# Second sums ahead of the seventh weight step, placed queries rounded behind the eighth

## The chip, the cores and the metric

The kernel runs on one core of one Trainium2 chip. The metric is the device time of one execution in microseconds (us). Its engines are TensorE (PE; PEld is its weight load), VectorE (DVE), ScalarE (ACT), GpSimd (POOL) and SyncE (SP); the last two are used here almost only to issue transfers.

## The reference, cut to what matters

A trunk of four layers works on x of 256 positions by 2048 features, in float32. Each layer has one mixer of the kinds 0, 1, 2, 0. Kinds 1 and 2 are the "grouped" layers that the change concerns: 32 query heads share 4 key and value heads of width 64; kind 1 attends to 64 selected keys per query, kind 2 to a window of 128.

```python
h = _rmsnorm(x, norm_in[i])
self_out, mq, gate = mixer(h @ w_in)                  # 2048 wide, 1024, 3072
mem_out = _memory_attention(mq, mem_n @ w_mem_kv[i])  # 4 heads of 256
y = concat([self_out, mem_out]) * silu(gate)          # 3072 wide
x = x + y @ w_out[i]
```

## The kernel before

**Products in two halves.** Each float32 operand is split into a rounded high part and the rest. For a weight tile `wr` ScalarE writes `wh` (L58) and VectorE writes `wl` (L71), in `split_in_order`; TensorE then makes three products, x high by `wh`, x high by `wl`, x low by `wh` (L241 to L243 in `rows_by`). A "weight step" is 1024 columns of weights on 128 partitions (two contraction tiles of 512 columns): one transfer of 512 KB on SP's queue, one `wh`, one `wl` and 12 matmuls of 512 columns. A product over 2048 features takes eight steps, called s = 0, 2, 4, ..., 14 in the code; so s = 12 is the seventh and s = 14 the eighth. There are five buffers for `wr` and three each for `wh` and `wl`.

**The order of a grouped layer.** Parts are worked in the order 4, 0, 1, 2, 3, 5; parts 4 and 5 are the memory heads, parts 0 to 3 the four groups g of eight query heads. For a group: the queries (`rows_by` "q", eight steps), the gate (`gate_by_rows`, `rows_by` "gr", eight steps), then the output product of the part before (`w_out`, "wo", four chunks of two steps). The sums of values of a part are made while the part after it has its queries and its gate computed, in four pieces called `steps`: `parts(0)`, first sums, `parts(1)`, second sums. `parts` rounds the turned softmax weights (tiles `pL` and `vz`, with high part `pH`). The sums of one half are 12 matmuls into tile `o` (`mo` for the memory heads); `paired` (or `gated`) multiplies them by the gate on VectorE (`yt`) and splits the product on ScalarE and VectorE (`y`).

**Queries are placed through DRAM.** The query accumulators go through `qz`, `qT`, a transfer `placed<-qT` and eight transfers `qR<-placed`, all issued by POOL, four for each half z. `parts_q(z)` then rounds the placed half `qR` to `qS` (ScalarE, then VectorE on 64 partitions). Scores (`sp`, three matmuls of 256 columns for a head, six for a pair of heads) read `qS`; softmax, its transposes and POOL's transfers `turn<-T`, `pL<-turn`, `vz<-turn` follow.

**What sets the order.** The program is traced in Python order; a planner then orders the instructions of each engine by its own simulated times, and each engine runs its list strictly in that order. `tc.keep_in_program_order` keeps the planner from moving an instruction, and `tc.issue_after(ins)` puts an instruction behind `ins` on the same engine. `split_in_order` uses the list `behind`: the next `wh` and `wl` are issued after whatever stands in it. `hooks` of `rows_by` maps a step to functions that are traced behind that step's matmuls.

Before the change, the gate of a group had these hooks (L965, L966), and `parts_q` put both halves into `behind`:

```python
hooks = {2: [lambda: behind.extend(ahead)], 10: steps[2:3], 12: steps[3:] + [lambda: parts_q(0), pairs[0]],
         14: [lambda: parts_q(1)] + pairs[1:]}
```

So second sums and the rounding of the first placed half were traced behind step 12, and the `wh` of step 14 was issued behind the latter. Where the second sums' matmuls fell among those of the weight steps was left to the planner.

Of the kernel before, what the change touches and what calls it, by code (L numbers as in the profile page):

```python
# [15 lines left out]
P = 128  # L16
S = 256
# [15 lines left out]
def kernel(ctx: ExitStack, tc: tile.TileContext, a: dict, out: bass.AP,  # L33
                             kinds=(0, 1, 2, 0)):
    nc = tc.nc
# [28 lines left out]
    behind = []  # L64
# [156 lines left out]
    def accumulators(name):  # L221
        return ps.tile([P, 2, 512], F32, name=f"acc_{name}", tag="acc", bufs=2)

    def rows_by(xt, kts, w, k0, cols, name, hooks={}, opening=False):

        acc = accumulators(name)
        n = cols[1] if len(cols) == 2 else cols[1] * cols[4]
        step = 4 if n <= 256 else ST
        for s in range(0, kts, step):
            wr, n = stage(w, k0 + s, step, cols)  # L230
            if opening:
                for f in hooks[s]:
                    f()
            wh, wl = parts_of(wr, step * n, n if opening and s < 8 else None)
            for k in range(step):
                q = xt[(s + k) // 4]
                at = slice(k * n, (k + 1) * n)
                for t in range(2):
                    xh, xl = (q[:, v, (s + k) % 4, t * P:(t + 1) * P] for v in range(2))
                    first, last = s + k == 0, s + k == kts - 1  # L240
                    nc.tensor.matmul(acc[:, t, :n], xh, wh[:, at], start=first, stop=False)  # L241
                    nc.tensor.matmul(acc[:, t, :n], xh, wl[:, at], start=False, stop=False)  # L242
                    nc.tensor.matmul(acc[:, t, :n], xl, wh[:, at], start=False, stop=last)  # L243
            for f in () if opening else hooks.get(s, ()):
                f()
        return acc
# [213 lines left out]
            copy_act(dst(i0, i1), f32(tp)[:, :(i1 - i0) * P].rearrange("p (j c) -> p j c", c=P))  # L460


    def gate(nm, w, c0, hooks={}):
        gT = None
        for h in range(2):
            z = total(columns_by(nm.at, 16, w, 0, (c0 + h * S, S), "g", {} if h else hooks))
            if gT is None:
                gT = act.tile([P, 4, S], F32, name="gT", tag="gT", bufs=1)
            nc.vector.tensor_mul(z, z, nm.half[:, None, :].to_broadcast([P, 2, S]))
            th = gT[:, 2 * h:2 * h + 2, :]  # L470
            nc.scalar.activation(th, z, AF.Tanh)
            nc.vector.scalar_tensor_tensor(th, th, 1.0, z, op0=OP.add, op1=OP.mult)
        return gT


    def gate_by_rows(nm, w, c0, hooks={}):
        acc = rows_by(nm.at, 16, w, 0, (c0, 512), "gr", hooks)
        gT = act.tile([P, 8, 4, 32], F32, name="gTr", tag="gT", bufs=1)
        d = dr.tile([2, P, 512], F32, name="turned", tag="turned", bufs=4)
        for t in range(2):  # L480
# [127 lines left out]
    def memory_project(nm, i, w, mq0, g0, part, steps, deferred):  # L608
# [7 lines left out]
        for h in range(2):  # L616
# [12 lines left out]
            head_parts(q, acc)  # L629
            qT.append(q)  # L630
        return (nm, kT, v, qT), lambda: gate(
            nm, w, g0 + 2048 + part * 512, {8: steps[2:3], 12: steps[3:]} if deferred else {})

    def memory_attend(nm, kT, v, qT):
        ws = []
# [25 lines left out]
        def sums(h, y, gT, p_s):  # L661
            pH, pL = p_s
            o = misc("mo")
            for j in range(2):
                c = (2 * h + j) * P
                seq = [(v[z][:, t, c:c + P], p_[:, t * S:(t + 1) * S])
                       for t in range(2) for z, p_ in ((0, pH), (0, pL), (1, pH))]
                for n_, (l, r_) in enumerate(seq):
                    nc.tensor.matmul(o[:, j * S:(j + 1) * S], l, r_, start=n_ == 0, stop=n_ == 5)
            gated(y, o, gT, 2 * h)  # L670
        return Sums([ws[:1], ws[1:]], lambda h, y, gT, p_s: sums(h, y, gT, p_s[0]))


# [158 lines left out]
    class Grouped:  # L832
# [108 lines left out]
        def project(self, g, steps):  # L941
# [14 lines left out]
            def parts_q(z):  # L956
                r4 = raw[z][:].rearrange("p (t m b) -> p m t b", m=4, b=32)
                one = tc.keep_in_program_order(copy_act(quads(q[z]), r4))
                two = nc.vector.tensor_sub(quads(q[z])[64:], r4[64:], quads(f32(q[z]))[64:])
                behind.extend((one.ins, two.ins))  # L960
            if g == 0:
                self.load_biases(0, 0)
                self.load_biases(0, 1)
            pairs, sums = self.attend(g, q)
            hooks = {2: [lambda: behind.extend(ahead)], 10: steps[2:3], 12: steps[3:] + [lambda: parts_q(0), pairs[0]],  # L965
                     14: [lambda: parts_q(1)] + pairs[1:]}  # L966
            if g < 3:
                for s_, half in ((4, 0), (14, 1)):
                    hooks.setdefault(s_, []).append(lambda half=half: self.load_biases(g + 1, half))
            return sums, gate_by_rows(nm, self.w, self.g0 + g * 512, hooks)  # L970

        def load_biases(self, g, half):
            bm = act.tile([P, 4, S], F32, name="bm", tag="aux", bufs=AUX)
# [9 lines left out]
        def attend(self, g, q):  # L983
# [28 lines left out]
            def sums(z, y, gT, p_s):  # L1012
                o = misc("o")
                for u in range(2):
                    pp = p_s[u]
                    v0 = g * P + (64 if u == 0 else 0)
                    for t in range(2):
                        for n_, (x_, p_) in enumerate(((0, 0), (0, 1), (1, 0))):
                            nc.tensor.matmul(o[:, t * S:], self.vz[x_][:, t, v0:v0 + P],
                                             pp[p_][:, 512 * t:512 + 256 * t],  # L1020
                                             start=u == t == n_ == 0, stop=u == t == 1 and n_ == 2)
                paired(y, o, gT, 2 * z)
            order = (0, 2, 1, 3, 4, 6, 5, 7)

            def pair(m):
# [197 lines left out]
```

## Time and profile before

| | |
|---|---|
| median of 3 runs | 2578.14 us (2577.4 to 2580.79) |
| the profiled execution | 2578.37 us, of which the span from first to last instruction is 2576.6 us |
| TensorE busy | 2531.9 us, 98% of the span |
| mean granted TensorE clock | 0.992 |
| VectorE, ScalarE, POOL busy | 71%, 55%, 16% |
| HBM traffic | 236 GB/s over the span |

Busy shares are means over stages with different limits. In the rows below a time is us from the span's start, the second number of a timeline row is its length in us, and square brackets hold the idle time of the engine ahead of the row and what ended it. A clock of 1.00 is 2.4 GHz, the lower level is 1.2 GHz, and a value between says that a stretch holds both.

### The profile page before, as it was taken

Reading aid. Unit: us, or ns where it says so; the run is one execution under the profiler, and the core shown is the slowest. Engines: PE = TensorE matmul, PEld = TensorE weight load, DVE = VectorE, ACT = ScalarE, POOL = GpSimd, SP = SyncE. Lnnn points to the kernel's source line nnn. Section 1 sums busy time; section 2 is a strip of 40 time slices with the busy share of each in tenths; the row PEclk is TensorE's granted clock in tenths of the full one; section 3 lists DMA queues with packets and bytes.
Section 4 is the critical chain, followed back from the end, with each engine's and each line's share of the span. In section 5 each row is a group of like instructions: output and inputs, shape, how many; then the busy total and the mean of one; then the engine's idle time right before and its main releaser. Section 6 shows DMA issues by size and latency. Waiting matters only on the chain.

```text
span 2576.6 us, 38117 instructions
## 1 busy us (share of the span) xinstructions
PE 2531.9 (98%) x13336; PEld 2176.3 (84%) x13336; DVE 1823.0 (71%) x3074; ACT 1418.0 (55%) x2236; POOL 402.5 (16%) x649
## 2 busy tenths in 40 slices
PE   8999999999999999999999999999999999999998
PEld 7888888888888889877787888777788888888887
DVE  6565656677676685877787775877787667777767
ACT  6454546555455454556566554665565555455554
POOL 1000000111111100112332101222230011111110
PEclk9999999999999999999999999999999999999999
DMA  9889888877887757678888677788894887888874
GB/s 311 275 276 310 279 283 242 211 208 206 222 224 229 217 175 210 204 217 246 265 270 231 203 240 213 244 244 236 255 255 149 243 210 207 210 220 219 249 214 151
DMA packets 462399, 597.26 MB, mean 232 GB/s; under 512 B 78768, under 2 KB 306752, under 8 KB 461056
## 3 DMA queue, kind: packets, MB, share of 16 engines
q1 hardware_dynamic: 419856, 464.46, 60.3%
q0 software_dynamic: 41344, 129.47, 17.9%
q8 instruction: 105, 1.72, 0.3%
q10 hardware_dynamic: 1008, 0.91, 0.1%
q14 instruction: 86, 0.70, 0.1%
HBM read 536.30 MB, written 71.01 MB: 236 GB/s over the span
## 4 chain that ended last, share of the span: by engine, by line
PE 93%; DMA 4%; issue 1%; DVE 1%; POOL 1%; ACT 1%; ACTq 0%; SPq 0%; DVEq 0%; POOLq 0%
PE acc_wo L242 7%; PE acc_wo L243 7%; PE acc_wo L241 7%; PE acc_mq L265 5%; PE acc_mk L265 5%; PE acc_g L265 5%; PE acc_gr L242 4%; PE acc_gr L241 4%; PE acc_gr L243 4%; PE acc_cq L265 3%; PE acc_qn L265 3%; PE acc_mv L241 2%; PE acc_mq L267 2%; PE acc_g L267 2%; PE acc_mv L242 2%; PE acc_mk L267 2%
## 5 line engine op out<-in xcount | busy, mean ns | idle before, releaser
L71 DVE TENSOR_TENSOR wl<-wr,wh 128x1024 fp32r<-128x1024 f32 (+2 forms) x860 | 1028.2, 1197 | 539.5 <-ACT wh L58 530.1
L58 ACT ACTIVATE wh<-wr 128x1024 fp32r<-128x1024 f32 (+2 forms) x860 | 891.2, 1038 | 837.8 <-PE acc_wo L243 167.8
L241 PE MATMUL acc_wo<-wh,y 128*128 128x512 f32 x752 | 293.5, 390 | 0.0
L242 PE MATMUL acc_wo<-wl,y 128*128 128x512 f32 x752 | 293.5, 390 | 0.0
L243 PE MATMUL acc_wo<-wh,y 128*128 128x512 f32 x752 | 293.4, 390 | 0.0
L241 PE MATMUL acc_gr<-wh,xT 128*128 128x512 f32 x512 | 206.6, 403 | 26.7 <-ACT wh L58 26.7
L242 PE MATMUL acc_gr<-wl,xT 128*128 128x512 f32 x512 | 205.3, 401 | 1.3 <-DVE wl L71 1.3
L243 PE MATMUL acc_gr<-wh,xT 128*128 128x512 f32 x512 | 205.1, 401 | 0.0
L241 PEld LDWEIGHTS acc_wo<-wh,y 128*128 128x128 f32 x752 | 141.3, 188 | 29.0
L242 PEld LDWEIGHTS acc_wo<-wl,y 128*128 128x128 f32 x752 | 141.3, 188 | 28.2
L243 PEld LDWEIGHTS acc_wo<-wh,y 128*128 128x128 f32 x752 | 141.2, 188 | 27.8
L265 PE MATMUL acc_mq<-xT,wh 128*128 128x512 f32 x512 | 162.0, 396 | 0.0
L265 PE MATMUL acc_g<-xT,wh 128*128 128x512 f32 x512 | 161.4, 395 | 0.0
L265 PE MATMUL acc_mk<-mT,wh 128*128 128x512 f32 x512 | 160.8, 395 | 0.0
L544 POOL DMA_DIRECT2D pL<-turn x192 | 120.7, 635 | 201.9 <-DMA turn<-T 95.8
L241 PEld LDWEIGHTS acc_gr<-wh,xT 128*128 128x128 f32 x512 | 99.8, 195 | 48.5 <-ACT wh L58 28.3
L1127 DVE TENSOR_TENSOR x<-x,acc_wo 128x1024 f32<-128x1024 f32 x92 | 111.7, 1214 | 17.5 <-PE acc_wo L243 17.5
L539 POOL DMA_DIRECT2D turn<-T x56 | 42.7, 763 | 502.5 <-DVE T L533 468.9
L265 PE MATMUL acc_qn<-cT,wh 128*128 128x512 f32 x384 | 120.6, 395 | 0.0
L265 PE MATMUL acc_cq<-xT,wh 128*128 128x512 f32 x384 | 120.6, 395 | 0.0
L242 PEld LDWEIGHTS acc_gr<-wl,xT 128*128 128x128 f32 x512 | 100.0, 195 | 22.3 <-DVE wl L71 2.3
L243 PEld LDWEIGHTS acc_gr<-wh,xT 128*128 128x128 f32 x512 | 99.2, 194 | 20.3
(331 smaller groups left out, 5327.1 us busy)
## 6 DMA issues: line engine op xcount, KB each, us to landing
wr<-in_w_out_dram SPq DMA_DIRECT2D x192, 512.0 KB, 4.6
wr<-in_w_in_a_dram SPq DMA_DIRECT2D x176, 512.0 KB, 4.5
wr<-in_w_mem_kv_dram SPq DMA_DIRECT2D x128, 512.0 KB, 5.6
wr<-in_w_in_b_dram SPq DMA_DIRECT2D x116, 512.0 KB, 4.8
wr<-in_w_in_c_dram SPq DMA_DIRECT2D x104, 512.0 KB, 5.0
wr<-in_w_uq_dram SPq DMA_DIRECT2D x288, 128.0 KB, 3.9
turn<-T POOLq DMA_DIRECT2D x40, 384.0 KB, 5.4
tab<-flat POOLq DMA_DIRECT2D x8, 1536.0 KB, 11.7
```

Of the source, the lines that this page charges most:

```text
L58: return nc.scalar.activation(o, i, AF.Copy, scale=scale)
L71: two = nc.vector.tensor_sub(lo, src, f32(hi))
L241: nc.tensor.matmul(acc[:, t, :n], xh, wh[:, at], start=first, stop=False)
L242: nc.tensor.matmul(acc[:, t, :n], xh, wl[:, at], start=False, stop=False)
L243: nc.tensor.matmul(acc[:, t, :n], xl, wh[:, at], start=False, stop=last)
L265: nc.tensor.matmul(acc[j], wh[:, at[j]], q[:, :, kt % 4, :], start=first, stop=False)
L267: nc.tensor.matmul(acc[j][:, 0, :], wl[:, at[j]], q[:, 0, kt % 4, :], start=False, stop=last)
L539: nc.gpsimd.dma_start(d.rearrange("m p w -> p m w"), self.T.rearrange("p m j n b -> p m (j n b)"))
L544: nc.gpsimd.dma_start(f32(self.raw)[j * 32:(j + 1) * 32, :].rearrange("p (i r) -> p i r", r=r), bass.AP(tensor=d.tensor, offset=d.offset + ...
L1127: nc.vector.tensor_add(xs, xs, acc)
```

## The change

- `rows_by` has a new argument `between`: functions that are traced ahead of a step's matmuls, behind the rounding of its weights. Each returns its last matmul, and the step's matmuls are issued after it on TensorE.
- In the gate of a grouped layer's parts 0 to 3, `parts(1)` and the second sums (`steps[2:]`) move from the hooks of steps 10 and 12 to `between` of step 12.
- `parts_q(0)` and the first pair of heads (`pairs[0]`) move from the hook of step 12 to that of step 14, where `parts_q(1)` and the other pairs are. Only half 0 goes into `behind`, so the weights that are rounded behind it are those of the first step of the output product.
- In the gate of part 5 (memory heads, by columns in two halves of four steps), `parts(1)` moves from behind the third step to behind the fourth, and the second sums from behind the fourth step to behind the first step of the second half.

```diff
--- before.py
+++ after.py
@@ -221,7 +221,7 @@
     def accumulators(name):
         return ps.tile([P, 2, 512], F32, name=f"acc_{name}", tag="acc", bufs=2)
 
-    def rows_by(xt, kts, w, k0, cols, name, hooks={}, opening=False):
+    def rows_by(xt, kts, w, k0, cols, name, hooks={}, opening=False, between={}):
 
         acc = accumulators(name)
         n = cols[1] if len(cols) == 2 else cols[1] * cols[4]
@@ -232,15 +232,20 @@
                 for f in hooks[s]:
                     f()
             wh, wl = parts_of(wr, step * n, n if opening and s < 8 else None)
-            for k in range(step):
-                q = xt[(s + k) // 4]
-                at = slice(k * n, (k + 1) * n)
-                for t in range(2):
-                    xh, xl = (q[:, v, (s + k) % 4, t * P:(t + 1) * P] for v in range(2))
-                    first, last = s + k == 0, s + k == kts - 1
-                    nc.tensor.matmul(acc[:, t, :n], xh, wh[:, at], start=first, stop=False)
-                    nc.tensor.matmul(acc[:, t, :n], xh, wl[:, at], start=False, stop=False)
-                    nc.tensor.matmul(acc[:, t, :n], xl, wh[:, at], start=False, stop=last)
+            with ExitStack() as held:
+                for f in between.get(s, ()):
+                    ins = f()
+                    if ins is not None:
+                        held.enter_context(tc.issue_after(ins))
+                for k in range(step):
+                    q = xt[(s + k) // 4]
+                    at = slice(k * n, (k + 1) * n)
+                    for t in range(2):
+                        xh, xl = (q[:, v, (s + k) % 4, t * P:(t + 1) * P] for v in range(2))
+                        first, last = s + k == 0, s + k == kts - 1
+                        nc.tensor.matmul(acc[:, t, :n], xh, wh[:, at], start=first, stop=False)
+                        nc.tensor.matmul(acc[:, t, :n], xh, wl[:, at], start=False, stop=False)
+                        nc.tensor.matmul(acc[:, t, :n], xl, wh[:, at], start=False, stop=last)
             for f in () if opening else hooks.get(s, ()):
                 f()
         return acc
@@ -460,10 +465,10 @@
             copy_act(dst(i0, i1), f32(tp)[:, :(i1 - i0) * P].rearrange("p (j c) -> p j c", c=P))
 
 
-    def gate(nm, w, c0, hooks={}):
+    def gate(nm, w, c0, hooks):
         gT = None
         for h in range(2):
-            z = total(columns_by(nm.at, 16, w, 0, (c0 + h * S, S), "g", {} if h else hooks))
+            z = total(columns_by(nm.at, 16, w, 0, (c0 + h * S, S), "g", hooks[h]))
             if gT is None:
                 gT = act.tile([P, 4, S], F32, name="gT", tag="gT", bufs=1)
             nc.vector.tensor_mul(z, z, nm.half[:, None, :].to_broadcast([P, 2, S]))
@@ -473,8 +478,8 @@
         return gT
 
 
-    def gate_by_rows(nm, w, c0, hooks={}):
-        acc = rows_by(nm.at, 16, w, 0, (c0, 512), "gr", hooks)
+    def gate_by_rows(nm, w, c0, hooks={}, between={}):
+        acc = rows_by(nm.at, 16, w, 0, (c0, 512), "gr", hooks, False, between)
         gT = act.tile([P, 8, 4, 32], F32, name="gTr", tag="gT", bufs=1)
         d = dr.tile([2, P, 512], F32, name="turned", tag="turned", bufs=4)
         for t in range(2):
@@ -629,7 +634,7 @@
             head_parts(q, acc)
             qT.append(q)
         return (nm, kT, v, qT), lambda: gate(
-            nm, w, g0 + 2048 + part * 512, {8: steps[2:3], 12: steps[3:]} if deferred else {})
+            nm, w, g0 + 2048 + part * 512, ({12: steps[2:3]}, {0: steps[3:]}) if deferred else ({}, {}))
 
     def memory_attend(nm, kT, v, qT):
         ws = []
@@ -666,8 +671,9 @@
                 seq = [(v[z][:, t, c:c + P], p_[:, t * S:(t + 1) * S])
                        for t in range(2) for z, p_ in ((0, pH), (0, pL), (1, pH))]
                 for n_, (l, r_) in enumerate(seq):
-                    nc.tensor.matmul(o[:, j * S:(j + 1) * S], l, r_, start=n_ == 0, stop=n_ == 5)
+                    one = nc.tensor.matmul(o[:, j * S:(j + 1) * S], l, r_, start=n_ == 0, stop=n_ == 5)
             gated(y, o, gT, 2 * h)
+            return one.ins
         return Sums([ws[:1], ws[1:]], lambda h, y, gT, p_s: sums(h, y, gT, p_s[0]))
 
 
@@ -957,17 +963,18 @@
                 r4 = raw[z][:].rearrange("p (t m b) -> p m t b", m=4, b=32)
                 one = tc.keep_in_program_order(copy_act(quads(q[z]), r4))
                 two = nc.vector.tensor_sub(quads(q[z])[64:], r4[64:], quads(f32(q[z]))[64:])
-                behind.extend((one.ins, two.ins))
+                if z == 0:
+                    behind.extend((one.ins, two.ins))
             if g == 0:
                 self.load_biases(0, 0)
                 self.load_biases(0, 1)
             pairs, sums = self.attend(g, q)
-            hooks = {2: [lambda: behind.extend(ahead)], 10: steps[2:3], 12: steps[3:] + [lambda: parts_q(0), pairs[0]],
-                     14: [lambda: parts_q(1)] + pairs[1:]}
+            hooks = {2: [lambda: behind.extend(ahead)],
+                     14: [lambda: parts_q(0), pairs[0], lambda: parts_q(1)] + pairs[1:]}
             if g < 3:
                 for s_, half in ((4, 0), (14, 1)):
                     hooks.setdefault(s_, []).append(lambda half=half: self.load_biases(g + 1, half))
-            return sums, gate_by_rows(nm, self.w, self.g0 + g * 512, hooks)
+            return sums, gate_by_rows(nm, self.w, self.g0 + g * 512, hooks, {12: steps[2:]})
 
         def load_biases(self, g, half):
             bm = act.tile([P, 4, S], F32, name="bm", tag="aux", bufs=AUX)
@@ -1016,10 +1023,12 @@
                     v0 = g * P + (64 if u == 0 else 0)
                     for t in range(2):
                         for n_, (x_, p_) in enumerate(((0, 0), (0, 1), (1, 0))):
-                            nc.tensor.matmul(o[:, t * S:], self.vz[x_][:, t, v0:v0 + P],
+                            one = nc.tensor.matmul(o[:, t * S:], self.vz[x_][:, t, v0:v0 + P],
                                              pp[p_][:, 512 * t:512 + 256 * t],
                                              start=u == t == n_ == 0, stop=u == t == 1 and n_ == 2)
+                            last = one.ins
                 paired(y, o, gT, 2 * z)
+                return last
             order = (0, 2, 1, 3, 4, 6, 5, 7)
 
             def pair(m):
```

## Rows read from the trace of the kernel before

**Rows 1.** The page, part 1: busy time, share of span, instructions.
```profile
PE 2531.9 (98%) x13336; PEld 2176.3 (84%) x13336; DVE 1823.0 (71%) x3074; ACT 1418.0 (55%) x2236; POOL 402.5 (16%) x649
```

**Rows 2.** The waits of TensorE: total, times, longest.
```profile
PE acc_gr L241 <- ACT wh L58: 26.7, 8, 3.3
...
PE acc_gr L242 <- DVE wl L71: 1.3, 5, 0.3
```

**Rows 3.** Timeline of TensorE, end of the last group's gate in layer 2.
```profile
1850.76 0.50 PE L241 MATMUL acc_gr<-wh,xT 128*128 128x512 f32 x1 [3.34 <-ACT wh L58]
...
1852.33 0.64 PE L242 MATMUL acc_gr<-wl,xT 128*128 128x512 f32 x1 [0.21 <-DVE wl L71]
...
1856.54 0.40 PE L241 MATMUL acc_wo<-wh,y 128*128 128x512 f32 x1
```

**Rows 4.** Timeline of ScalarE, ends of the last two groups' gates, layer 2.
```profile
1772.39 1.06 ACT L58 ACTIVATE qS<-qR 128x1024 fp32r<-128x1024 f32 x1 [0.41 <-DMA qR<-placed]
...
1848.18 0.63 ACT L58 ACTIVATE y<-yt 128x512 fp32r<-128x512 f32 x1 [7.25 <-DVE yt L512]
1848.72 1.04 ACT L58 ACTIVATE qS<-qR 128x1024 fp32r<-128x1024 f32 x1
1849.67 1.04 ACT L58 ACTIVATE wh<-wr 128x1024 fp32r<-128x1024 f32 x1
1852.61 1.06 ACT L58 ACTIVATE qS<-qR 128x1024 fp32r<-128x1024 f32 x1 [1.90 <-DMA qR<-placed]
1853.57 1.04 ACT L58 ACTIVATE wh<-wr 128x1024 fp32r<-128x1024 f32 x1
```

**Rows 5.** Timeline of VectorE, the last group's gate.
```profile
1840.01 0.96 DVE L552 TENSOR_TENSOR vz<-vz,pH 128x768 fp32r<-128x768 f32 x1 [2.34 <-ACT pH L58]
```

**Rows 6.** Windows, TensorE, stall's end to output product: busy, clock, DMA.
```profile
1130.49:1136.27 5.78, 5.49 (x19) 0.70 0.47 158
...
sum 47.36, PE 46.07; mean PE 5.76
```

**Rows 7.** Timeline of TensorE, three other gates, layers 1 and 2.
```profile
1208.85 0.51 PE L241 MATMUL acc_gr<-wh,xT 128*128 128x512 f32 x1 [3.34 <-ACT wh L58]
...
1693.36 0.79 PE L241 MATMUL acc_gr<-wh,xT 128*128 128x512 f32 x1 [3.34 <-ACT wh L58]
...
1762.37 0.39 PE L243 MATMUL acc_gr<-wh,xT 128*128 128x512 f32 x1
...
1763.73 0.39 PE L243 MATMUL acc_gr<-wh,xT 128*128 128x512 f32 x1
...
1772.04 0.50 PE L241 MATMUL acc_gr<-wh,xT 128*128 128x512 f32 x1 [3.34 <-ACT wh L58]
```

**Rows 8.** Timeline of VectorE: the last rounding ahead of the second sums, two gates.
```profile
1199.48 0.96 DVE L552 TENSOR_TENSOR vz<-vz,pH 128x768 fp32r<-128x768 f32 x1 [1.88 <-ACT pH L58]
...
1762.37 0.96 DVE L552 TENSOR_TENSOR vz<-vz,pH 128x768 fp32r<-128x768 f32 x1 [3.42 <-ACT pH L58]
```

**Rows 9.** The chain of waits: start, length, what.
```profile
1674.52 7.20 DMA placed<-qT
...
1686.06 6.37 DMA qR<-placed
```

**Rows 10.** The waits of POOL in 1600 to 1870, one row.
```profile
POOL pL L544 <- DMA turn<-T: 14.0, 2, 7.3
```

**Rows 11.** Windows, an output product: length, PE, PEld, DVE, ACT, POOL, clock, DMA.
```profile
1699.00:1723.00 24.00, 24.00 (x112) 20.00 (x111) 21.91 (x54) 16.11 (x36) 6.67 (x11) 1.00 0.80 233
```

**Rows 12.** Timeline of TensorE, layer 0.
```profile
627.40 0.47 PE L241 MATMUL acc_va<-wh,cT 128*128 128x512 f32 x1 [0.81 <-DVE qn L292]
```

**Rows 13.** Windows, TensorE, the stretch behind that row.
```profile
627.40:630.40 3.00, 3.00 (x13) 1.00 0.24 41
```

**Rows 14.** Timeline of ScalarE in the gate of part 5, layer 1.
```profile
1441.61 0.63 ACT L58 ACTIVATE y<-yt 128x512 fp32r<-128x512 f32 x1 [3.62 <-DVE yt L512]
...
1448.42 0.58 ACT L58 ACTIVATE z<-acc_g 128x512 f32<-128x512 f32 x1
```

## The prediction

> **What bounds the kernel now.** I read the page first: TensorE is busy 98% of the span [rows 1], so only what it waits for or does slowly can be won. Then its waits: 26.7 us in eight equal pieces of 3.3 in front of a grouped gate's matmuls, released by ScalarE's `wh`, and 1.3 us more on `wl` [rows 2]. Then the timelines around one of them. TensorE has nothing from 1847.42 (1850.76 less 3.34) to 1850.76 [rows 3], and ScalarE shows why: it sits idle for 7.25 us until the product `yt` of the second sums exists, then makes `y`, rounds the first placed half `qS` at 1848.72 and only then rounds the weights of the eighth step, 1849.67 to 1850.71 [rows 4]. The `wh` that TensorE lacks could have been made in those 7.25 us; it stands in the queue behind `qS`, and `qS` behind the sums. The other gates show the same 3.34 [rows 7], as the same chain of instructions must.
>
> The idle time is not the whole price. From the end of each stall to the output product takes 47.36 us over the eight gates, at a mean granted clock of 0.70 in the first window, which holds both 2.4 and 1.2 GHz [rows 6]. The work there is 12 matmuls of 512 columns and six of half that width. Six matmuls at the full clock take 1.36 us (1762.37 to 1763.73), 0.227 each [rows 7]; so a weight step is 2.72, the six scores 0.68, together 3.40, and eight times that is 27.2. The eight stretches lose 20.2 us, 2.5 each, the 1.3 of `wl` included. The stake is 26.7 + 20.2 = 46.9 us, 5.9 for a gate.
>
> **The change part by part.** *Second sums ahead of the seventh step.* No instruction is added; 12 matmuls, 6 x 0.227 + 6 x 0.113 = 2.04 us, move ahead of 2.72 us of weight step. TensorE ends both at the moment at which it ends them now; the sums are ready 2.72 earlier, and `yt`, `y` and `qS` run beside the seventh step. The new wait: TensorE's queue now holds at the sums until the last `pL` or `vz` is rounded, with the seventh and eighth steps behind it. It wants them 4.76 (2.04 + 2.72) before the stall begins today. In three gates that is 1200.75, 1763.94 and 1842.66 (stalls begin at 1205.51, 1768.70, 1847.42 [rows 3, 7]); the rounding ends at 1200.44, 1763.33 and 1840.97 [rows 5, 8]. Margins are 0.3, 0.6 and 1.7 us, and the other five have more. I cost the wait at nothing; if the transfers come later it is that much (rivals).
>
> *Rounding behind the eighth step.* The `wh` of the eighth step no longer stands behind `qS`; the 7.25 idle us of ScalarE hide it [rows 4]. That removes the stall, both its 3.34 and the slow stretch. What is late next is the first step of the output product: its `wh` now stands behind `qS` of half 0, and I take ScalarE's order to stay first half, second half, `wh`, with the eighth step's `wh` out of it [rows 4]. TensorE wants this `wh` 3.40 us after the moment at which it stalls today. The first half costs nothing: in the last gate it would start at 1847.42 - 2.72 + 1.30 = 1846.0 if its data were there and starts at 1848.72 today; even then two more operations of about 1 us end at 1850.7, against 1850.82 wanted. The second half waits for its transfer: `qS` starts at 1852.61, released by `qR`, and the `wh` behind it ends at 1854.61, 3.8 late [rows 4]. One gate earlier it starts at 1772.39 [rows 4], the `wh` ends two operations later (0.96 + 1.04) at 1774.39, wanted at 1772.10: 2.3 late. In layer 2's second gate `qR` lands at 1692.43 [rows 9], the `wh` would end at 1694.43, wanted at 1693.42: 1.0 late. Sum 7.1 us. The rows bound this from both sides: nothing, if the planner puts that `wh` ahead of the second half, and 7.1 plus 3.0 in each gate if the transfers slip as well (second rival).
>
> Does TensorE's clock fall after such a short wait? Behind 3.34 us it does in all eight gates [rows 6]; behind 0.81 us the next 3 us have a clock of 1.00 [rows 12, 13]. The 3.8 is nearest to the first, so I charge it 2.5, and the 1.0 and 2.3 nothing. The Trainium skill, "TensorE: Matmul & The Clock Gate", section "HAM oscillation — how this bites in real kernels", says that idle gaps between bursts of matmuls throttle the clock again and that the price is paid each time; read so for all three waits, the sum would be 5.0 us higher, 2546.
>
> *The pairs of heads* move with the rounding: the first pair's scores, its softmax and its `turn`, `pL`, `vz` transfers on POOL. Queries of half 0 are rounded earlier than today, so the pair does not start later in time; against the output product's first step it does (below). The bias loads on SP's queue keep their place. *Part 5*: `y` starts at 1441.61 and the gate's last accumulators are read at 1448.42 [rows 14]; a step of 2.7 later still leaves over 4 us, and no wait of TensorE lies there. Nothing.
>
> **Sum.** The profiled execution took 2578.37, its span 2576.6, the median 2578.14; I work from the first. 2578.37 - 46.9 + 7.1 + 2.5 = 2541.1.
>
> **The rivals.** *All of it is won.* The planner sees `qR` late and rounds the output weights first. For it: the eighth `wh` stood ahead of the second half in today's queue [rows 4]. Against it: it was the tracing order that put it there. 2578.37 - 46.9 = 2531.5.
>
> *Layer 2 becomes a loop of transfers.* Today `qS` starts 7.82 us before the output product's first matmul (1848.72 to 1856.54 [rows 3, 4]); afterwards 4.82 (2.72 - 1.30 + 3.40). The softmax starts 3.0 later against the weight steps, and VectorE, busy 21.91 of 24 us there [rows 11], can hardly catch up. Then everything that POOL sends comes 3.0 later: the three tight sums wait 2.7, 2.4 and 1.3, and the three late output steps 4.0, 2.9 and 5.5, each less what the sums of its gate have waited: 18.8 us, and three slow stretches, 7.5. 2531.5 + 26.3 = 2557.8. The Trainium skill, "DMA: Bandwidth & Descriptors", section "Issuing engines are not separate DMA queues", has all queues share the same 16 engines. By it, packing a gate of 78.7 us into 5.9 less (7.5%) also lengthens `placed` and `qR`, 7.20 and 6.37 us [rows 9], by about 1.0 together: an estimate of 3 us over three gates, 2544.
>
> *Nothing changes.* ScalarE's list keeps the eighth `wh` behind `y` for the planner's own reasons. 2578.
>
> *Slower.* TensorE waits at the sums in every gate that follows a group, because a turn's transfer lands late: POOL has waited up to 7.3 us for one [rows 10]. At 7.3 in six gates, with a slow stretch each, 6 x 9.8 = 58.8 outweighs 46.9: 2590. It decides once the eight waits average over 5.9 us; the tightest margin is +0.3, so transfers would have to slip by over 6.
>
> **How the numbers follow.** Forecast 0.44, all of it 0.24, the loop 0.20, nothing 0.05, slower 0.07. The range from 2531 to 2561 takes in the first three and leaves out 0.12 and a little of their edges. 0.2% is 5.2 us, about what a measurement can tell from no change: faster 0.88, same 0.05, slower 0.07.
>
> **What the profile after would show.** Right: no 3.3 us waits of `acc_gr` on `wh`; `o` matmuls in a block ahead of the seventh step; the eighth `wh` ahead of `y` on ScalarE; waits of 1 to 4 us on `wh` in front of `acc_wo`, in layer 2 alone. Wrong: waits in front of `o` on `pL` or `vz` (second and last rival), waits of `acc_wo` in layer 1, or the eighth `wh` still behind `qS`.

## The result, and the profile after

The changed kernel took 2536.77 us (median of 4, 2532.95 to 2539.76) against 2577.98 for the kernel before beside it (median of 4, 2577.4 to 2580.79): a ratio of 0.9837, 95% interval 0.982 to 0.9854. The profiled execution is the longest of the four, 2539.76 us, span 2538.0, mean granted clock 0.999.

The page of the kernel after, part 1, answers to [rows 1]:

```profile
PE 2514.0 (99%) x13336; PEld 2164.5 (85%) x13336; DVE 1823.1 (72%) x3074; ACT 1418.8 (56%) x2236; POOL 403.8 (16%) x649
```

The instructions of every engine are as many as before. The span fell by 38.6 us (2576.6 to 2538.0): 17.9 in which TensorE is busy (2531.9 to 2514.0, the same 13336 matmuls) and 20.7 in which it is idle (44.7 to 24.0). The first part is the slow clock behind the stalls, the second the stalls less what has come in their place. What has come is in the waits of TensorE, kernel after (total, times, longest), to be read against [rows 2]:

```profile
PE acc_mv L246 <- ACT wh L58: 7.0, 1, 7.0
PE o L1026 <- ACT pH L58: 5.4, 3, 2.2
PE acc_va L246 <- DVE qn L297: 1.7, 2, 1.4
PE o L1026 <- DVE vz L557: 1.0, 2, 0.5
PE acc_wo L247 <- DVE wl L71: 0.4, 1, 0.4
```

The first row is the start of the kernel, 7.0 before as well. The 26.7 of `acc_gr` on `wh` are gone, and so is its 1.3 on `wl`; new are 6.4 us in front of the sums (`o`) and 0.4 in front of the output product. With `acc_va`, 1.7 where it was 1.1, in another part of the program, that is -28.0 + 6.8 + 0.6 = -20.6, the idle time that went. (L246 to L248 are L241 to L243 of before, L1026 was L1019.)

The last gate of layer 2 shows the new order. Timeline of TensorE, kernel after:

```profile
1805.06 0.39 PE L248 MATMUL acc_gr<-wh,xT 128*128 128x512 f32 x1
1805.29 0.39 PE L1026 MATMUL o<-pH,vz 128*128 128x512 f32 x1
...
1807.25 0.28 PE L1026 MATMUL o<-pH,vz 128*128 128x256 f32 x1
1807.37 0.40 PE L246 MATMUL acc_gr<-wh,xT 128*128 128x512 f32 x1
...
1812.63 0.39 PE L248 MATMUL acc_gr<-wh,xT 128*128 128x512 f32 x1
1812.86 0.28 PE L998 MATMUL sp<-kd,qS 128*128 128x256 f32 x1
...
1813.57 0.40 PE L246 MATMUL acc_wo<-wh,y 128*128 128x512 f32 x1
```

The sums stand in one block of 2.08 us (1805.29 to 1807.37), then come the seventh and eighth steps without a gap, 5.49 us for 24 matmuls, the first pair's scores and the output product. Nothing waits, and the window from 1805.06 to 1812.86 has a clock of 1.00. ScalarE beside it, timeline of the kernel after, answers to [rows 4]:

```profile
1804.53 0.85 ACT L58 ACTIVATE pH<-vz 128x768 fp32r<-128x768 f32 x1 [2.68 <-DMA vz<-turn]
1805.28 1.05 ACT L58 ACTIVATE wh<-wr 128x1024 fp32r<-128x1024 f32 x1
1808.96 1.06 ACT L58 ACTIVATE qS<-qR 128x1024 fp32r<-128x1024 f32 x1 [2.63 <-DMA qR<-placed]
1809.92 1.04 ACT L58 ACTIVATE wh<-wr 128x1024 fp32r<-128x1024 f32 x1
1813.16 0.63 ACT L58 ACTIVATE y<-yt 128x512 fp32r<-128x512 f32 x1 [2.20 <-DVE yt L517]
...
1828.06 1.04 ACT L58 ACTIVATE qS<-qR 128x1024 fp32r<-128x1024 f32 x1
```

The `wh` of the eighth step (1805.28) is made ahead of `qS` and `y`, while TensorE works at the sums. The `wh` of the output product's first step (1809.92) stands directly behind half 0 of the queries, and half 1 comes only at 1828.06, 19 us after half 0, behind the first pair's softmax and several more `wh`. The prediction had half 1 ahead of that `wh`. It also had `y` ahead of half 0, as in [rows 4]; here half 0 starts 4.2 us ahead of `y` (1808.96 and 1813.16), and it stands ahead of `y` in all eight gates. That, too, is a place in ScalarE's list that the text of the change does not write out.

Where the new waits are: timeline of TensorE in layer 2, kernel after, the rows with a wait (second and third gate, output product behind the last gate, and the first sums of part 3):

```profile
1657.75 0.49 PE L1026 MATMUL o<-pH,vz 128*128 128x512 f32 x1 [1.65 <-ACT pH L58]
1658.75 0.50 PE L1026 MATMUL o<-vz 128*128 128x512 f32 x1 [0.50 <-DVE vz L557]
...
1732.91 0.49 PE L1026 MATMUL o<-pH,vz 128*128 128x512 f32 x1 [1.58 <-ACT pH L58]
1733.90 0.50 PE L1026 MATMUL o<-vz 128*128 128x512 f32 x1 [0.50 <-DVE vz L557]
...
1826.03 0.50 PE L247 MATMUL acc_wo<-wl,y 128*128 128x512 f32 x1 [0.39 <-DVE wl L71]
...
1864.80 0.50 PE L1026 MATMUL o<-pH,vz 128*128 128x512 f32 x1 [2.19 <-ACT pH L58]
```

ScalarE's row for the first of them, kernel after, says what was late, a turned `vz` on its way through DRAM:

```profile
1656.86 0.84 ACT L58 ACTIVATE pH<-vz 128x768 fp32r<-128x768 f32 x1 [5.39 <-DMA vz<-turn]
```

### The profile page after: what moved, and what is told of

It is laid out like the page before. It is cut to its first block, busy times and chain, and to the rows that moved or that the text cites. A ratio compares the mean times of both kernels' runs of the same rounds, so it can differ in the third digit from the quotient of the medians.

```text
span 2538.0 us, 38103 instructions
## 1 busy us (share of the span) xinstructions
PE 2514.0 (99%) x13336; PEld 2164.5 (85%) x13336; DVE 1823.1 (72%) x3074; ACT 1418.8 (56%) x2236; POOL 403.8 (16%) x649
## 4 chain that ended last, share of the span: by engine, by line
PE 93%; DMA 3%; DVE 1%; POOL 1%; issue 1%; ACT 0%; SPq 0%; ACTq 0%; POOLq 0%; DVEq 0%
PE acc_wo L247 7%; PE acc_wo L248 7%; PE acc_wo L246 7%; PE acc_g L270 5%; PE acc_mk L270 5%; PE acc_mq L270 4%; PE acc_gr L246 4%; PE acc_gr L247 4%; PE acc_gr L248 4%; PE acc_cq L270 4%; PE acc_qn L270 3%; PE acc_mv L246 2%; PE acc_g L272 2%; PE acc_mk L272 2%; PE acc_mv L247 2%; PE acc_mv L248 2%
## 5 line engine op out<-in xcount | busy, mean ns | idle before, releaser
L246 PE MATMUL acc_wo<-wh,y 128*128 128x512 f32 x752 | 293.4, 390 | 0.0
L248 PE MATMUL acc_wo<-wh,y 128*128 128x512 f32 x752 | 293.3, 390 | 0.0
L247 PE MATMUL acc_gr<-wl,xT 128*128 128x512 f32 x512 | 199.7, 390 | 0.0
L246 PE MATMUL acc_gr<-wh,xT 128*128 128x512 f32 x512 | 199.6, 390 | 0.0
L248 PE MATMUL acc_gr<-wh,xT 128*128 128x512 f32 x512 | 199.5, 390 | 0.0
L246 PEld LDWEIGHTS acc_wo<-wh,y 128*128 128x128 f32 x752 | 141.3, 188 | 28.7
L248 PEld LDWEIGHTS acc_wo<-wh,y 128*128 128x128 f32 x752 | 141.2, 188 | 28.4
L272 PEld LDWEIGHTS acc_mk<-mT,wl 128*128 128x128 f32 x512 | 96.2, 188 | 22.7
L272 PEld LDWEIGHTS acc_g<-xT,wl 128*128 128x128 f32 x512 | 96.1, 188 | 22.0
L272 PEld LDWEIGHTS acc_mq<-xT,wl 128*128 128x128 f32 x512 | 95.6, 188 | 21.6
```

Source lines behind the costliest of these rows:

```text
L272: nc.tensor.matmul(acc[j][:, 0, :], wl[:, at[j]], q[:, 0, kt % 4, :], start=False, stop=last)
```

## The experiments

All kernels compute the whole reference. Ratios are to the kernel before, run beside them on the same chip (2582.2 us for the first four below, 2581.5 for the next four, 2581.2 for the last two). The change has two halves that can be told apart: TensorE's order (sums ahead of the seventh step) and ScalarE's order (queries behind the eighth). The theory of the prediction: the eighth `wh` stood behind `qS`, `qS` behind the sums, and either cut of this chain frees it. The rivals: the fixed order of TensorE is what counts; or the turns of layer 2 come late and set the time that is left. The times expected below were worked out against 2578 us, so ratios are the safer comparison.

**Only the queries moved.** Second sums traced where they were, rounding behind the eighth step, part 5 as before.

```diff
-            hooks = {2: [lambda: behind.extend(ahead)],
+            hooks = {2: [lambda: behind.extend(ahead)], 10: steps[2:3],
+                     12: steps[3:],
                      14: [lambda: parts_q(0), pairs[0], lambda: parts_q(1)] + pairs[1:]}
...
-            return sums, gate_by_rows(nm, self.w, self.g0 + g * 512, hooks, {12: steps[2:]})
+            return sums, gate_by_rows(nm, self.w, self.g0 + g * 512, hooks)
```

> Only the second half of the change: the placed queries are rounded behind the eighth weight step and only half 0 goes into the list; second sums stay in the hooks of steps 10 and 12, and part 5 is as before. Theory 'freed weights': the 46.9 us came from rounding the eighth step's weights behind the placed queries, which stand behind the sums; with that gone the sums may end late without TensorE noticing, and they come 2.7 us later than in the changed kernel, so its three waits at the sums of the groups (4.2 us) shrink too: 2532 to 2538 us, no wait of acc_gr on wh. Rival 'order': the sums must end earlier for the chain to be hidden; then the wait moves to the output product's first step and the time is 2560 or more.

Measured 2539.11 us, ratio 0.9838 (0.9822 to 0.9854): the whole gain, from this half alone (1 us more than the range that was expected). The waits of TensorE in this kernel:

```profile
PE acc_gr L246 <- ACT wh L58: 2.4, 1, 2.4
PE o L1027 <- ACT pH L58: 0.9, 1, 0.9
```

Seven of the eight gates have no wait on `wh` left. The last gate of layer 2 has one of 2.4, which was not expected. Its cause is in ScalarE's timeline of the same kernel:

```profile
1801.01 0.84 ACT L58 ACTIVATE pH<-vz 128x768 fp32r<-128x768 f32 x1 [7.10 <-DMA vz<-turn]
1801.76 1.99 ACT L58 ACTIVATE wh<-wr 128x1024 fp32r<-128x1024 f32 x2
```

A weight rounding is again queued behind something it does not need, this time behind `pH`, which waited 7.10 us for a turn.

The sums of this kernel end where they ended before, behind the seventh step. What changed beside the eighth `wh` is the place of the queries. ScalarE in its first gate of layer 1:

```profile
1120.47 1.06 ACT L58 ACTIVATE qS<-qR 128x1024 fp32r<-128x1024 f32 x1 [0.97 <-DMA qR<-placed]
...
1126.08 0.64 ACT L58 ACTIVATE y<-yt 128x512 fp32r<-128x512 f32 x1
```

Half 0 runs 5.6 us ahead of `y` as soon as its transfer lands, although it is traced a step later than before. So the late sums hold up neither the queries nor the weights that stand behind them.

**Only the sums moved.** Sums ahead of the seventh step, rounding and list as before, part 5 as before.

```diff
-                if z == 0:
-                    behind.extend((one.ins, two.ins))
+                behind.extend((one.ins, two.ins))
...
-            hooks = {2: [lambda: behind.extend(ahead)],
-                     14: [lambda: parts_q(0), pairs[0], lambda: parts_q(1)] + pairs[1:]}
+            hooks = {2: [lambda: behind.extend(ahead)], 12: [lambda: parts_q(0), pairs[0]],
+                     14: [lambda: parts_q(1)] + pairs[1:]}
```

> Only the first half of the change: second sums stand ahead of the seventh step and TensorE's order is fixed; both halves of the queries are rounded behind the seventh and the eighth step and go into the list, as before; part 5 is as before. Theory 'freed weights': the eighth step's wh is still behind qS, but the sums end 2.7 us earlier, so of each wait of 3.34 us some 0.6 stays, too short for the slow clock; with 1.0, 2.3 and 3.8 us less 0.6 each in front of the output product in layer 2, and the waits at the sums: 2542 to 2552 us. If the sums' place were without effect: 2578. If it did everything: 2537.

Measured 2552.65 us, ratio 0.9893 (0.9877 to 0.991). The chain is only started earlier, by the 2.72 of a weight step, so 3.34 - 2.72 = 0.6 of each stall should remain. Waits of TensorE in this kernel, and one of its rows:

```profile
PE acc_gr L246 <- ACT wh L58: 5.6, 8, 1.3
PE acc_gr L247 <- DVE wl L71: 2.1, 8, 0.3
...
PE acc_wo L247 <- DVE wl L71: 1.7, 5, 0.6
```

```profile
1202.70 0.50 PE L246 MATMUL acc_gr<-wh,xT 128*128 128x512 f32 x1 [0.61 <-ACT wh L58]
```

Eight waits again, 5.6 / 8 = 0.7 on average, 0.59 to 0.61 in seven gates and 1.34 in the last one of layer 2. The two halves of the change overlap and don't add: this one gives 1.07%, the other 1.62%, both together 1.63%.

**Both halves of the queries in the list.** The changed kernel with its one new condition taken out, so that the output product's first weights are rounded behind both halves.

```diff
-                if z == 0:
-                    behind.extend((one.ins, two.ins))
+                behind.extend((one.ins, two.ins))
```

> The changed kernel with both halves of the placed queries in the list, so that the output product's first weights are rounded behind the second half as well. As my forecast assumed ScalarE's order (first half, second half, weights): waits of 1.0, 2.3 and 3.8 us in layer 2 alone, some 2545 us. The rival reads the tracing order: the second half stands behind the first pair's softmax, so the weights wait for two heads, about 11 us in each of eight gates with a slow stretch behind each: 2600 to 2660 us, slower than before the change.

Measured 2616.48 us, ratio 1.0137 (1.0122 to 1.0152), slower than the kernel before. Waits of TensorE in this kernel, then its ScalarE ahead of a wait of 4.22 (TensorE's output product begins at 1139.79):

```profile
PE acc_wo L246 <- ACT wh L58: 31.7, 8, 4.2
PE sp L997 <- DVE mn L585: 19.0, 16, 2.5
```

```profile
1137.04 0.80 ACT L58 ACTIVATE u<-u,rc 128x128 f32<-128x128 f32 x2 [0.86 <-DVE rc L607]
1137.75 1.04 ACT L58 ACTIVATE qS<-qR 128x1024 fp32r<-128x1024 f32 x1
1138.70 2.93 ACT L58 ACTIVATE wh<-wr 128x1024 fp32r<-128x1024 f32 x3
```

Here the order is that of the text of the program: half 0, first pair with its softmax (`u`), half 1, and only then `wh`, three of them in a row. So half 1 does not stand beside half 0 on ScalarE, as the prediction took it; it stands behind the pair. The rival named ahead of the run had this order. The single `if z == 0` is worth 1.0137 - 0.9837 = 3.0% of the time before, 77 us (the medians differ by 79.7, but the kernel before beside this one was itself 4 us slower than the one beside the change).

**Both halves ahead of all pairs.** Traced in the order that the prediction assumed.

```diff
-                     14: [lambda: parts_q(0), pairs[0], lambda: parts_q(1)] + pairs[1:]}
+                     14: [lambda: parts_q(0), lambda: parts_q(1)] + pairs}
```

> The changed kernel with the second half rounded straight behind the first, ahead of the first pair's scores (only half 0 is in the list). Theory 'late softmax': in the changed kernel the second half is rounded some 19 us behind the first (1828.06 against 1808.96), which makes the last turn late and TensorE wait at the second sums in layer 2 (1.65, 1.58 and 0.5 twice) and in part 5 (2.19); with it early these waits of 6.4 us shrink to under 2 and the time to 2530 to 2535. Rival 'transfers': the waits come from the transfers of POOL and from VectorE, which the order of the halves doesn't touch: 2535 to 2540, the waits stay.

Measured 2541.15 us, ratio 0.9843 (0.9826 to 0.986), not to be told from the change. The waits at the second sums of the groups are gone, but two others are there, waits of TensorE in this kernel:

```profile
PE o L1026 <- ACT pH L58: 4.9, 2, 3.5
PE acc_wo L247 <- DVE wl L71: 3.1, 5, 0.9
```

On ScalarE half 1 now starts 3.4 to 5.1 us behind half 0 in all eight gates; ahead of the output product's first `wh` it stands in only two of them, the first of each layer. The new waits lie at a first sum of layer 2 (1784.22, 1.42 us) and at part 5's (1865.04, 3.46 us). The waits moved; together with the 3.1 us in front of the output product, 8.0 us, the waits are not below the 6.8 of the changed kernel.

**Sums ahead of the eighth step instead of the seventh.**

```diff
-            return sums, gate_by_rows(nm, self.w, self.g0 + g * 512, hooks, {12: steps[2:]})
+            return sums, gate_by_rows(nm, self.w, self.g0 + g * 512, hooks, {14: steps[2:]})
```

> The changed kernel with the second sums ahead of the eighth weight step instead of the seventh. They are wanted 2.7 us later, so the waits of 4.2 us at the sums of the groups vanish; but y now stands ahead of the placed queries on ScalarE, which stand ahead of the output product's first weights, all behind the sums' end 2.7 us ahead of the gate's end: yt, y, qS, wh end about 4.2 us behind the sums, against 2.7 + 0.7 wanted, so 0.8 to 1.5 us of wait in each of eight gates, 6 to 12 together: 2538 to 2546 us. If only the waits at the sums counted: 2533.

Measured 2544.05 us, ratio 0.9856 (0.9842 to 0.9869). Waits of TensorE in this kernel:

```profile
PE acc_wo L246 <- ACT wh L58: 4.8, 8, 0.6
PE acc_wo L247 <- DVE wl L71: 2.1, 8, 0.3
```

No wait at the sums is left, since the turns have 2.7 us more, but the chain from sums to `y` now ends that much later: 0.6 + 0.26 us in each of eight gates in front of the output product. In this kernel `y` stands ahead of half 0 again, in all eight gates, as expected.

**Parts of the change taken back one at a time.** No fixed order behind the sums; part 5 as before; the bias loads of the next group, which go out on SP's queue, both behind the eighth step (one was behind the third).

```diff
-                    if ins is not None:
-                        held.enter_context(tc.issue_after(ins))
```

> The changed kernel without the fixed order: the second sums are traced ahead of the seventh step's matmuls, but these may be issued before them, as the planner likes. Theory 'freed weights': TensorE's order has no effect by itself, the planner will spread the sums over the seventh step and the waits at the sums get no longer: 2531 to 2538 us. Rival 'order': without it the sums end late, and the chain behind them comes back as waits in front of the output product: over 2545 us.

```diff
-            nm, w, g0 + 2048 + part * 512, ({12: steps[2:3]}, {0: steps[3:]}) if deferred else ({}, {}))
+            nm, w, g0 + 2048 + part * 512, ({8: steps[2:3], 12: steps[3:]}, {}) if deferred else ({}, {}))
```

> The changed kernel with part 5's gate as before the change (last rounding behind the third step, second sums behind the fourth of its first half). I costed this edit at nothing: 2534 to 2540 us, the same as the changed kernel; the wait of 2.19 us in part 5 belongs to the first sums and stays. If the edit carried part of the gain: 2542 or more.

```diff
-                for s_, half in ((4, 0), (14, 1)):
+                for s_, half in ((14, 0), (14, 1)):
```

> The changed kernel with the first bias load of a gate (bm, 512 KB) issued behind the eighth step, beside the second, and not behind the third. Theory 'shared transfers': TensorE waits 1.65 + 0.50 and 1.58 + 0.50 us at the second sums of the two middle gates of layer 2, because vz lands 7.1 us after its issue there, and not in the last gate, where no bias is loaded and it takes 5.6; with the load out of the way the waits of these two gates fall under 1 us together, the wait in part 5 (2.19) stays, and the time falls by 2 to 4 us. Rival 'late softmax': the last turn is late by itself, the bias load has no part in it, waits and time stay. A third possibility: the bias lands too late for the next group's scores, and the time rises.

Measured 2536.22 (ratio 0.9827, 0.9813 to 0.984), 2536.54 (0.9827, 0.9813 to 0.9841) and 2537.58 (0.9832, 0.9817 to 0.9847): all three like the change itself. Without the fixed order the planner spreads the sums over the seventh step. TensorE in the last gate of layer 2 of that kernel:

```profile
1801.40 0.39 PE L1024 MATMUL o<-pH,vz 128*128 128x512 f32 x1
...
1803.44 0.39 PE L1024 MATMUL o<-pL,vz 128*128 128x512 f32 x1
```

One matmul of the sums comes first, eight of the step's twelve follow, and the other eleven of the sums run from 1803.44 to 1805.30. So the sums end 8 x 0.227 = 1.8 us later against the weight steps than in one block, and the kernel takes the same time: the written order has no effect of its own that can be measured. The edit of part 5 is worth nothing. The waits at `o` in these kernels were 2.3; 1.8 + 0.5; and 1.7 + 0.7 us, where the changed kernel had 5.4 + 1.0. With the bias loads later, the two gates that were expected to wait less have 0.2 us left of 4.2, but the last gate, where no bias is loaded, waits 1.40 + 0.50, and the fall of 2 to 4 us did not come. Since the second kernel has the bias loads where they were and waits no more than the third, the later bias loads can't be said to have helped: this test is inconclusive.

**The kernel before with the list alone edited.** Only half 1 is put into `behind`, nothing is moved.

```diff
-                behind.extend((one.ins, two.ins))
+                if z == 1:
+                    behind.extend((one.ins, two.ins))
```

> The kernel before the change with one edit: half 0 of the placed queries is no longer put into the list, half 1 still is. So the eighth step's weights are free, the sums stay where they were, and the output product's first weights stand behind both halves, first half, second half, weights, the order that my forecast assumed. Theory 'freed weights': the waits of 3.34 us of acc_gr vanish and most of the gain is there; what is late next is the output product: scores that need qS and weights behind two roundings come some 1 to 3 us late in each gate, 12 to 28 us together, and up to 3.8 in layer 2 for the second half's transfer: ratio 0.986 to 0.993 to the kernel before. If the sums' or the queries' place in the trace carried the gain: 1.00.

Measured 2565.96 us (median of 6), ratio 0.9944 (0.9927 to 0.9961), less gain than the 0.986 to 0.993 that was expected. The stalls of 3.34 are gone here too. Waits of TensorE in this kernel, then ScalarE in its first gate of layer 1 (before, the `wh` stood behind the first `qS`):

```profile
PE sp L992 <- DVE qS L959: 7.6, 8, 1.0
...
PE acc_wo L242 <- DVE wl L71: 6.0, 8, 0.8
PE sp L992 <- DVE mn L580: 4.5, 8, 0.6
```

```profile
1121.58 1.06 ACT L58 ACTIVATE wh<-wr 128x1024 fp32r<-128x1024 f32 x1 [1.66 <-PE acc_gr L243]
1129.22 0.63 ACT L58 ACTIVATE y<-yt 128x512 fp32r<-128x512 f32 x1 [6.58 <-DVE yt L503]
1129.75 1.99 ACT L58 ACTIVATE qS<-qR 128x1024 fp32r<-128x1024 f32 x2
1131.65 1.99 ACT L58 ACTIVATE wh<-wr 128x1024 fp32r<-128x1024 f32 x2
```

The eighth step's `wh` is out of the queue behind `qS`, but sums, `y` and queries come as late as before, and now scores and output product wait for them, 1.0 and 0.8 us at most in each gate. So freeing the eighth `wh` alone gives 0.6%, a third of the gain. This kernel differs from "only the queries moved" in two things: half 0 stands behind `y`, and the output product's weights stand behind both halves; which of the two costs more was not tested apart.

The place of half 0 goes with the result in all the kernels. It is ahead of `y` in all eight gates of every kernel at 0.983 to 0.984. It is behind `y` in "only the sums moved" (0.9893), "sums ahead of the eighth step" (0.9856) and here (0.9944). "Both halves in the list" is the one kernel that has it ahead of `y` and loses, since its weights wait for half 1. No run moved half 0 alone, so this is a pattern and not a test.

**The last three edits together** (no fixed order, part 5 as before, bias loads later).

> The changed kernel without the fixed order, with part 5 as before and the first bias load behind the eighth step. Each of these left the time where it was, by itself, and what TensorE still waits for differs between executions by more than any of them; so the same as the changed kernel, ratio 0.982 to 0.984. If their parts added up: 0.981 or less.

Measured 2535.71 us, ratio 0.9828 (0.9813 to 0.9844): no gain beside the change. Its waits at `o` are 4.8 us, 4.2 of them in part 5. Among the kernels with the sums ahead of or in the seventh step, the size and the place of what is left differ from one to the next and don't follow the edits.

## Why the prediction was right, and which step failed

*The stake* (46.9 us) was right in its mechanism and close in size. The stalls of [rows 3, 7] are gone in all eight gates. "Only the sums moved" shows the chain itself, since what it leaves is what the prediction's 2.72 leaves of 3.34. The slow stretches of [rows 6] were named at 20.2 us, 18.9 without the 1.3 of `wl`, which was idle time. TensorE's busy time bears them out: it fell by 17.9 us for the same matmuls. The slow stretch behind the new 2.19 us wait, below, takes an estimated 5.2 x (1 - 0.67) = 1.7 us of that, so about 19.6 us were won.

*Sums ahead of the seventh step: no instruction more, both steps end when they did.* Right, the block takes 2.08 us where 2.04 was worked out, though "only the queries moved" and the kernel without the fixed order show that the place of the sums was not needed for the gain. That the new wait costs nothing was the weak point: the margins of 0.3 (layer 1) and 1.7 us (last gate of layer 2) held, that of 0.6 in the third gate of layer 2 didn't (1.58 + 0.50), and the second gate, which was among the five with more, waited 1.65 + 0.50.

*Rounding behind the eighth step: the failed step.* The prediction took ScalarE's order to stay "first half, second half, `wh`", and from it charged 3.8, 2.3 and 1.0 us of waits in front of the output product in layer 2 and 2.5 for a slow stretch, 9.6 in all. That term did not come: `acc_wo` waited 0.39 us once, on `wl`. The planner put the `wh` directly behind half 0, and half 1 19 us later, the lower bound ("nothing") of the prediction's own two. The prediction took `y` to stay ahead of half 0 as well, and half 0 now stands ahead of `y`. "List alone" has the order that was assumed, `y`, both halves, `wh`, with the sums as late as before, and there waits in front of scores and output product do come, in every gate. "Both halves in the list" shows that the order traced puts half 1 behind the first pair's softmax, so leaving the other half out of the list is not a detail: with it the change loses. In place of the term stand 6.4 us of waits at the sums and a slow stretch of 1.7. In the profiled execution, the longest of the four, 46.9 - 38.6 = 8.3 us were given back where 9.6 was forecast; by the medians it is 46.9 - 41.2 = 5.7. So the stake was understood, but that the time came out near 2541 is in part luck: a term of about the right size stood in another place.

*The rivals.* "All of it is won", 2531.5, was right about the order on ScalarE and is 5.3 us below the median. "A loop of transfers" was half right: the first group of its waits, in front of `o` on `pH` and `vz`, is there, and the late output steps are not. The 6.4 us are also what its 2.7, 2.4 and 1.3 add up to, but by chance: it put them in one gate of layer 1 and the last two of layer 2, and of these only the third gate of layer 2 waits. The prediction's own sign against itself ("waits in front of `o`") is thus in the trace. Its cause in the rival, a softmax that starts 3.0 us later against the weight steps, is not shown: "both halves ahead of all pairs" moved the waits to other sums and left the time. "Nothing" and "slower" are out; the latter needed over 5.9 us a gate, and the longest wait in front of a sum is 2.19.

*The clock behind short waits.* The prediction charged a slow stretch behind 3.8 us and none behind 2.3 and less. Windows of TensorE, kernel after, behind the waits of 1.65, 1.58 and 2.19 us (length, then the busy time of PE, PEld, DVE, ACT and POOL, then clock, DMA share and GB/s):

```profile
1657.75:1661.00 3.25, 2.75 (x12) 2.13 (x13) 2.16 (x2) 1.23 (x2) 0.00 (x0) 1.00 1.05 253
...
1864.80:1870.00 5.20, 5.20 (x22) 4.59 (x23) 5.07 (x10) 2.73 (x6) 2.72 (x5) 0.67 0.60 170
```

The same view of TensorE alone (length, busy time, clock, DMA share, GB/s), behind the waits of 1.40 and 0.50 us in the kernel with later bias loads, and behind one of 2.25 us in front of `acc_va` in the kernel with the last three edits:

```profile
1804.49:1809.69 5.20, 4.70 (x14) 0.67 1.05 234
...
2381.52:2386.72 5.20, 5.20 (x23) 1.00 0.84 238
```

Behind 1.65 the clock stays at 1.00 (behind 1.58 too), behind 2.19 it is 0.67 over the next 5.2 us. Ahead of all three TensorE was busy without a gap at 1.00 (windows of 5.3 to 6.1 us that end where the waits begin). Behind the 2.44 of "only the queries moved" the clock is 0.70 over 5.2 us. So a slow stretch was met behind shorter waits than the one that was charged. But the length of a single wait does not decide it: behind 1.40 and 0.50 the clock is 0.67, where behind 1.65 and 0.50 it stays at 1.00, and behind 2.25 it stays at 1.00 too. In "list alone" the same run of three waits (0.91, 0.59 and 0.75) is followed by 0.67 in the first gate of layer 1 and by 1.00 in the third. What decides it stays open. The Trainium skill, "TensorE: Matmul & The Clock Gate", section "HAM oscillation — how this bites in real kernels", has idle gaps between bursts throttle the clock, a price paid each time. Its example has longer waits than these; here the price was paid behind 2.19 and 2.44 us, and not behind 1.58, 1.65 and 2.25.

*What stays open* is why a turn lands late. The view of transfers gives the `vz<-turn` a median of 7.1 us from issue to landing in the window from 1721.5 to 1724.1 (third gate, which waits), and 5.6 from 1795.6 to 1798.2 (last gate, which doesn't):

```profile
vz<-turn POOLq DMA_DIRECT2D x4, 96.0 KB, 7.1
...
vz<-turn POOLq DMA_DIRECT2D x4, 96.0 KB, 5.6
```

The last gate has no bias load beside it, which fits the Trainium skill, "DMA: Bandwidth & Descriptors", section "Issuing engines are not separate DMA queues": all queues share the same 16 engines. But the window of the third gate also holds two weight loads where that of the last holds one; before the change such a transfer, with a bias load beside it, took 7.5 us and nobody waited; and moving the bias loads changed no time (6.7 us from issue to landing in the third gate). The waits at `o` of the kernels with the sums ahead of or in the seventh step and half 0 alone in the list, 2.3 to 6.4 us, differ also where the edit does not touch them, and one profile of each can't tell the edit from the landing of that execution.

## What to carry to other kernels

When an engine that runs its list in order holds up a busier one, look in its queue for the instruction ahead of the late one and ask whether the late one needs it; then ask the same of the instruction that it stood behind. Here taking the weights alone out of the way gave 0.6% (with a cost of its own, since other weights then stood behind both halves), making the chain ahead of them shorter 1.1%, and letting the queries run ahead of `y` as well 1.6%; adding the shorter chain to that gave nothing. An entry in a list of "issue this first" is part of such a change: with one entry too many the same kernel was slower than before. Count a stall with the slow stretch behind it, and count an ordering on another engine as unknown, from nothing to the full wait, until a trace shows it.

## What the runs showed of the hardware

The granted clock of TensorE stayed at 1.00 behind idle gaps of 1.58, 1.65 and 2.25 us, and fell to a mean of 0.67 over the 5.2 us behind one of 2.19 us, and behind two of 1.40 and 0.50 us with one matmul between them. The length of the gap alone did not tell which it would be. Of the 38.6 us by which the span fell, 17.9 were not idle time at all but the same matmuls at a higher clock.
